# Attention scores from plain float32 queries and keys: two heads on the two row halves of the array, computed as one unit

## The chip, the cores and the metric

The kernel runs on one core of a Trainium2 chip. The metric is device time in microseconds, from the first to the last instruction of an execution and the little around it. The kernel before takes 2615.68 us (median of 3 executions, 2612.95 to 2617.23).

## The reference

One layer of a streaming encoder. 1024 frames of a new stream and 8 x 16 frames of running streams (together T = 1152 tokens, 9 tiles of 128) go through

    x = x + 0.5 * SwiGLU_1(RMSNorm(x))
    P = RMSNorm(x) @ w_in          # RWKV columns, and q, k, v of 8 attention heads of 64
    x = x + concat(RWKV7(P_rwkv), BandAttn(P_att)) @ w_out
    x = x + 0.5 * SwiGLU_2(RMSNorm(x));  y = RMSNorm_final(x)

What matters here is the attention. A chunk of 64 queries sees a band of keys, the 512 before it and its own 64:

    s = einsum('bhqd,bhkd->bhqk', q, k) * HEAD_DIM ** -0.5 + bias
    s = where(valid, s, -1e30);  p = softmax(s);  out = einsum('bhqk,bhkd->bhqd', p, v)

The running streams attend to a cache of 128 keys and to their own 16. Everything is float32; the last 512 keys and values are outputs as well. The RWKV part is a recurrence over time, so its chunks of 32 tokens must follow each other.

## The kernel before, in words

All large products are made in float32r, a float32 type that TensorE takes in one pass, with each operand split into a high part (rounded to float32r) and a low remainder; three products (high-high, high-low, low-high) stand for one.

The program has five stages. The first SwiGLU (lines 225 to 265). The projection `_project` (line 282), which for each of four pairs of heads projects the RWKV columns, prepares the RWKV chunks, and calls `_attention_in` (line 400) for that pair's q and k. Then `_attention_inputs` (line 355) projects v (`ps_av`, lines 377 to 379) while the RWKV recurrence already runs. Then attention and the rest of the recurrence side by side (lines 1167 to 1178). Then the output projection and the second SwiGLU.

`_attention_in` splits the projected q or k of a pair of heads (128 rows: two heads of 64) into high `qkh` (ScalarE, line 414) and low `qkl` (VectorE, line 415) and stores both to DRAM. A third, unsplit copy `qk` (VectorE, line 421) is made for the last third of q (the running streams) and the last two thirds of k; the keys that are an output are turned by TensorE into `ps_ko` (line 429) and copied out by ScalarE into `ko` (line 432).

`_attention_load` (line 881) loads a pair for attention, on GpSimd's DMA queue: per head a tile `kt` with the high part of the keys on rows 0 to 63 and the low part on rows 64 to 127, and tiles `q` of 384 tokens with the high part (and, apart, the low part) of the queries on both row halves. So the two float32r passes of line 941 contract over all 128 rows, and their sum is the full product. For the first pair the loads go in thirds.

An attention unit of the kernel before is one head and one tile of 128 queries, 72 in all (line 1014). `_attention_scores` (line 930) makes the scores `ps_s` in PSUM, adds the bias, takes the maximum (VectorE, line 963), the exponential `e` (ScalarE, line 966), and scales by the reciprocal sum (VectorE, line 968). `_attention_turn` (line 972) turns the probabilities by TensorE (`ps_pt`, line 980) and copies them to `ptr` on ScalarE. `_attention_out` (line 984) multiplies with v for both heads (`ps_o`, line 995). The units run in a software pipeline: scores of unit n, turn of unit n - 1, output of the pair before. The recurrence takes per chunk four groups of small products on TensorE: `ps_c` from `wout` (line 771), `ps_c` from `tt` (776), `ps_c` from `wst` (780, the new state) and `ps_yc` (784), with VectorE copies between (773, 778, 793).

The order on each engine isn't the order of the code: a scheduler puts the instructions of all these generators into one fixed list for each engine, which the engine works through in order. Pools of buffers add waits: a load into a buffer waits until its last reader is done. The SP queue carries the loads of weights and of the recurrence; GpSimd's queue carries attention's loads and stores, between GpSimd's own arithmetic for the recurrence (`y` at lines 833 and 841, `yo` at 853).

Of the kernel before, what the change touches and what calls it, by code (L numbers as in the profile page):

```python
# [395 lines left out]
def _attention_in(k, w, p, kind):  # L396
# [6 lines left out]
    def tile(dt, name):  # L403
        return k.io.tile([P, TG], dt, tag="ev", bufs=4, name=name)


    d = k.tc.dram_tile([2, 2, HD, T], F32, name=f"qk{kind}{p}")
    (k.kd if kind else k.qd)[p] = d
    for g in range(3):
        s = slice(g * TG, g * TG + TG)  # L410
# [19 lines left out]
        ko = tile(F32, "ko").rearrange("p (i h d) -> p i h d", h=2, d=HD)  # L430
        n = len(tiles)
        nc.scalar.activation(ko[:, :n].rearrange("p i h d -> p (i h d)"), tp[:, :n * P], AF.Copy)
# [442 lines left out]
def _attention_load(k, p):  # L875

    at = k.at
    dq = k.aq
    q = _K()

    q.ks = [at.tile([P, T], F32R, tag="kt", bufs=4, name="kt") for h in range(2)]
    q.v = at.tile([P, NT, P], F32, tag="v", bufs=2, name="v")

    q.bias = at.tile([P, 4, 256], F32, tag="bias", bufs=k.nbias, name="bias")
    q.qs = []
    for c in range(3):
        s = slice(TG * c, TG * c + TG)
        q.qs.append(at.tile([P, 2, 2, TG], F32R, tag="q", bufs=3, name="q"))
        for half in HEADS:
            dq.dma_start(q.qs[c][half].rearrange("d j h t -> d (j h) t").bitcast(F32),  # L890
                           k.qd[p][:, :, :, s].rearrange("j h d t -> d (j h) t"))
        if c == 0 or p == 0:
            cols = s if p == 0 else slice(0, T)
            for h in range(2):
                for j in range(2):
                    dq.dma_start(q.ks[h][HEADS[j], cols].bitcast(F32), k.kd[p][j, h, :, cols])
            i = slice(3 * c, 3 * c + 3) if p == 0 else slice(0, NT)
            dq.dma_start(q.v[:, i], k.vd[i, :, p * P:p * P + P].rearrange("i t d -> t i d"))
        if c == 0:
            dq.dma_start(q.bias, k.bias[p])  # L900
    return q


def _sample_load(k, p, a, q):
# [3 lines left out]
    qn = at.tile([P, 4, 2, NQ], F32, tag="qs", bufs=1, name="qs")  # L908
    k.aq.dma_start(qn.rearrange("p b e l -> p (b e l)"), k.qs[p])
    q.qz = at.tile([P, 4, 2, 2, NQ], F32, tag="z", bufs=1, name="qz")  # L910
    k.nc.gpsimd.memset(q.qz, 0.0)
    for e in range(2):
        k.nc.gpsimd.tensor_copy(q.qz[:, :, e, e], qn[:, :, e])
# [16 lines left out]
def _attention_scores(k, q, i, h):  # L930
# [4 lines left out]
    u = _K()  # L935
    u.q, u.i, u.h = q, i, h
    t = (i % 3) * P

    def scores(ps, c0, n):
        for j in range(2):  # L940
            mm(ps, q.qs[i // 3][:, j, h, t:t + P], q.ks[h][:, c0:c0 + n], start=j == 0, stop=j == 1)

    ps = k.psum.tile([P, 1024], F32, tag="s", bufs=2, name="ps_s")
    u.j0 = j0 = max(0, i - 4)
    if i < NPT:
        u.n = n = (i - j0 + 1) * P
        for c0 in range(0, n, 512):
            c1 = min(n, c0 + 512)
            scores(ps[:, c0:c1], j0 * P + c0, c1 - c0)
        w = min(n, 256)  # L950
        nc.vector.tensor_tensor(ps[:, n - w:n], ps[:, n - w:n], q.bias[:, h, 256 - w:], ALU.add)
        if i >= 4:
            nc.vector.memset(ps[64:128, 0:64], NEG)
    else:
        u.n = n = 2 * P
        for e in range(2):
            for b in range(4):
                mm(ps[32 * b:32 * b + 32, 0:P], q.qz[HEADS[h], b, e].rearrange("p e l -> p (e l)"),
                   q.kc[HEADS[h], 2 * b + e], start=e == 0, stop=e == 1)
        scores(ps[:, P:n], NPT * P, P)  # L960
        nc.vector.tensor_tensor(ps[:, :n], ps[:, :n], q.bias[:, 2 + h], ALU.add)
    nm = at.tile([P, 1], F32, tag="nm", bufs=4, name="nm")
    nc.vector.tensor_reduce(nm, ps[:, :n], AX.X, ALU.max, negate=True)
    u.e = at.tile([P, 5 * P], F32, tag="e", bufs=2, name="e")
    sm = at.tile([P, 1], F32, tag="sum", bufs=4, name="sum")
    nc.scalar.activation(u.e[:, :n], ps[:, :n], AF.Exp, bias=nm, accum_out=sm)
    nc.vector.reciprocal(sm, sm)
    nc.vector.tensor_scalar(u.e[:, :n], u.e[:, :n], sm, None, ALU.mult)
    return u
# [42 lines left out]
def _attention(k, a):  # L1012

    units = [(p, i, h) for p in range(NPAIR) for i in range(NT) for h in range(2)]
    done = []
    q = nq = None
    for n in range(len(units) + 2):
        if n < len(units):
            p, i, h = units[n]
# [221 lines left out]
```

## Time and profile before

| | us |
|---|---|
| median of 3 executions | 2615.68 |
| the profiled execution | 2614.86 |
| its span | 2613.1 |
| PE busy in it | 2508.2 (96%) |
| DVE busy | 1209.8 (46%) |
| ACT busy | 646.6 (25%) |
| GpSimd busy | 763.6 (29%) |

The span is read by stages. The two SwiGLU stages and the output projection (0 to 943 us and 1660 us to the end) hold nothing that the change touches. The stretch from 943 to 1261 us is the projection, 1261 to 1354 us that of v, 1354 to 1660 us attention beside the recurrence, of which the last 49 us (from 1611 us) are attention alone. TensorE's row says busy nearly everywhere, but the ends of its instructions are modelled, and its granted clock falls in the attention stretch, so there the starts of neighbouring instructions are the better measure of what one costs.

### The profile page before, as it was taken

To read this page: it belongs to the slowest core of one execution; us is meant where nothing else is said; L and a number is where in the kernel's file an instruction comes from. 1 tells how busy PE (TensorE), PEld (TensorE's weight loads), DVE (VectorE), ACT (ScalarE), POOL (GpSimd) and SP (SyncE) were. 2 spreads that over 40 slices of the span, in tenths; PEclk is the share of its full clock that TensorE was granted. 3 is DMA by queue.
4 is the path that set the end of the run, shared out by engine and by line. 5 is a ranking of instruction groups with operands and counts; after the bars stand their busy time and mean duration, and the time that the engine had idled before them with its cause. 6 is when DMAs were issued, how large, how long until landed. Compare 5 with 4: busy or idle time off the path is not lost.

```text
span 2613.1 us, 39575 instructions
## 1 busy us (share of the span) xinstructions
PE 2508.2 (96%) x16344; PEld 2270.1 (87%) x16344; DVE 1209.8 (46%) x2460; ACT 646.6 (25%) x1294; POOL 763.6 (29%) x686
## 2 busy tenths in 40 slices
PE   8999999999999899999997888899999999999998
PEld 8999999999999799989865666689999999999997
DVE  4432443244335443675856777513443344334435
ACT  5111111111111443344113345404111111111112
POOL 4222222222221343344114433103222222222221
PEclk9999999999999899999996889899999999999999
DMA  5311111111111234454669967301111111111111
GB/s 187 114 41 33 48 49 41 33 49 41 46 35 50 89 98 121 139 167 119 185 138 240 203 160 187 119 1 57 49 47 43 33 49 41 49 33 49 41 33 73
DMA packets 247798, 217.39 MB, mean 83 GB/s; under 512 B 54017, under 2 KB 218497, under 8 KB 247233
## 3 DMA queue, kind: packets, MB, share of 16 engines
q1 hardware_dynamic: 214252, 167.74, 22.1%
q0 software_dynamic: 7648, 25.43, 4.1%
q10 hardware_dynamic: 25716, 21.68, 2.7%
q8 instruction: 129, 2.11, 0.3%
q14 instruction: 53, 0.43, 0.1%
HBM read 155.35 MB, written 59.45 MB: 82 GB/s over the span
## 4 chain that ended last, share of the span: by engine, by line
PE 85%; DVE 6%; POOL 3%; issue 2%; ACT 1%; DMA 1%; SPq 0%; POOLq 0%; ACTq 0%; DVEq 0%
PE pg L218 7%; PE pg L220 7%; PE pg L219 7%; PE pu L218 7%; PE pu L220 7%; PE pu L219 7%; PE pd L256 7%; PE pd L258 7%; PE pd L257 7%; PE ps_p L220 2%; PE ps_p L219 2%; PE ps_p L218 2%; PE ps_wo L1071 1%; PE ps_wo L1070 1%; PE ps_wo L1069 1%
## 5 line engine op out<-in xcount | busy, mean ns | idle before, releaser
L156 POOL TENSOR_TENSOR spl<-raw,spl 128x1024 fp32r<-128x1024 f32 x166 | 399.5, 2409 | 796.8 <-ACT spl L155 796.7
L260 DVE TENSOR_TENSOR x<-pd,x 128x512 f32<-128x512 f32 x774 | 527.8, 691 | 7.0 <-PE pd L258 2.9
L244 DVE SCALAR_TENSOR_TENSOR hf<-pu,sl 128x384 f32<-128x384 f32 x132 | 73.6, 557 | 963.3 <-PE pu L220 949.0
L218 PE MATMUL pg<-xg,spl 128*128 128x384 f32 x1056 | 356.1, 337 | 0.0
L220 PE MATMUL pg<-xg,spl 128*128 128x384 f32 x1056 | 355.2, 336 | 0.0
L219 PE MATMUL pg<-xg,spl 128*128 128x384 f32 x1056 | 355.2, 336 | 0.0
L220 PE MATMUL pu<-xg,spl 128*128 128x384 f32 x1056 | 355.0, 336 | 0.0
L219 PE MATMUL pu<-xg,spl 128*128 128x384 f32 x1056 | 354.9, 336 | 0.0
L218 PE MATMUL pu<-xg,spl 128*128 128x384 f32 x1056 | 354.9, 336 | 0.0
L155 ACT ACTIVATE spl<-raw 128x1024 fp32r<-128x1024 f32 x166 | 174.8, 1057 | 628.5 <-PE pd L258 422.8
L256 PE MATMUL pd<-spl,h 128*128 128x512 f32 x792 | 310.6, 392 | 0.0
L258 PE MATMUL pd<-spl,h 128*128 128x512 f32 x792 | 310.4, 392 | 0.0
L257 PE MATMUL pd<-spl,h 128*128 128x512 f32 x792 | 310.4, 392 | 0.0
L247 POOL TENSOR_TENSOR h<-hf,h 128x384 fp32r<-128x384 f32 x132 | 134.1, 1016 | 589.3 <-ACT h L246 575.7
L218 PEld LDWEIGHTS pg<-xg,spl 128*128 128x128 f32 x1056 | 198.3, 188 | 1.8
L219 PEld LDWEIGHTS pg<-xg,spl 128*128 128x128 f32 x1056 | 198.4, 188 | 1.5
L220 PEld LDWEIGHTS pg<-xg,spl 128*128 128x128 f32 x1056 | 198.3, 188 | 0.0
L220 PEld LDWEIGHTS pu<-xg,spl 128*128 128x128 f32 x1056 | 198.2, 188 | 0.0
L218 PEld LDWEIGHTS pu<-xg,spl 128*128 128x128 f32 x1056 | 198.2, 188 | 0.0
L219 PEld LDWEIGHTS pu<-xg,spl 128*128 128x128 f32 x1056 | 198.2, 188 | 0.0
L258 PEld LDWEIGHTS pd<-spl,h 128*128 128x128 f32 x792 | 148.6, 188 | 33.7
L257 PEld LDWEIGHTS pd<-spl,h 128*128 128x128 f32 x792 | 148.5, 188 | 31.9
(227 smaller groups left out, 3656.0 us busy)
## 6 DMA issues: line engine op xcount, KB each, us to landing
raw<-in_w_ff_gate_dram SPq DMA_DIRECT2D x44, 512.0 KB
raw<-in_w_ff_up_dram SPq DMA_DIRECT2D x44, 512.0 KB
raw<-in_w_ff_down_dram SPq DMA_DIRECT2D x44, 512.0 KB
raw<-in_w_in_dram SPq DMA_DIRECT2D x26, 512.0 KB
q<-qk POOLq DMA_DIRECT2D x24, 384.0 KB, 8.0
ard<-ar SPq DMA_DIRECT2D x20, 256.0 KB
grd<-gram SPq DMA_DIRECT2D x20, 256.0 KB
wsd<-tb SPq DMA_DIRECT2D x20, 256.0 KB
```

The source lines that it names most:

```text
L155: k.nc.scalar.activation(dst[:, 0], raw, AF.Copy)
L156: k.nc.gpsimd.tensor_tensor(dst[:, 1], raw, dst[:, 0].bitcast(F32), ALU.subtract)
L218: mm(ps, w[:, 0, c], hi[:, c], start=c == 0, stop=False)
L219: mm(ps, w[:, 0, c], lo[:, c], start=False, stop=False)
L220: mm(ps, w[:, 1, c], hi[:, c], start=False, stop=c == KC - 1)
L244: nc.vector.scalar_tensor_tensor(hf, pu[:, :TG], 0.5, sl, ALU.mult, ALU.mult)
L247: nc.gpsimd.tensor_tensor(h[:, 1, s], hf, h[:, 0, s].bitcast(F32), ALU.subtract)
L256: mm(ps, ph[:, 0, a], pd[:, 0, b], start=j == 0, stop=False)
L257: mm(ps, ph[:, 0, a], pd[:, 1, b], start=False, stop=False)
L258: mm(ps, ph[:, 1, a], pd[:, 0, b], start=False, stop=j == len(pend) - 1)
L260: nc.vector.tensor_tensor(xs, ps, xs, ALU.add)
L1069: mm(ps, hi[:, c, s], ws[c][:, 0, b], start=c == 0, stop=False)
```

## The change

Queries and keys are no longer split. `_attention_in` makes one float32 tile `qk` on ScalarE, stores it once, and turns the output keys from the same tile; the copy of `ps_ko` moves to VectorE. `_attention_load` loads one tile of queries and one of keys for a pair of heads, head 0 on rows 0 to 63 and head 1 on rows 64 to 127; the tile of the running streams' queries is read from it, not loaded apart. `_attention_scores` makes both heads of a query tile in one unit: the code writes the two heads' products beside each other, each on its own 64 rows and into its own PSUM banks, and in plain float32 instead of two float32r passes. The probabilities `e` have 4 buffers instead of 2, q has 2 of 1152 tokens instead of 3 of 384 (split and doubled), kt 2 instead of 4.

```diff
 def _attention_in(k, w, p, kind):
...
-        hi, lo = tile(F32R, "qkh"), tile(F32R, "qkl")
-        nc.scalar.activation(hi, ps[:, :TG], AF.Copy, scale=scale)
-        nc.vector.scalar_tensor_tensor(lo, ps[:, :TG], scale, hi.bitcast(F32), ALU.mult, ALU.subtract)
-        for j, t in enumerate((hi, lo)):
-            k.aq.dma_start(d[j, :, :, s].rearrange("h d t -> (h d) t"), t.bitcast(F32))
-        if g == 0 or (g == 1 and kind == 0):
-            continue
-        raw = tile(F32, "qk")
-        nc.vector.tensor_scalar(raw, ps[:, :TG], scale, None, ALU.mult)
-        if kind == 0:
-            k.qs[p] = k.tc.dram_tile([P, P], F32, name=f"qs{p}")
-            k.aq.dma_start(k.qs[p], raw[:, 2 * P:])
+        raw = tile("qk")
+        nc.scalar.activation(raw, ps[:, :TG], AF.Copy, scale=scale)
+        k.aq.dma_start(d[:, g * TG:g * TG + TG], raw)
+        if g == 0 or kind == 0:
             continue
...
-        nc.scalar.activation(ko[:, :n].rearrange("p i h d -> p (i h d)"), tp[:, :n * P], AF.Copy)
+        nc.vector.tensor_copy(ko[:, :n].rearrange("p i h d -> p (i h d)"), tp[:, :n * P])
...
 def _attention_load(k, p):
...
-    q.qs = []
-    for c in range(3):
-        s = slice(TG * c, TG * c + TG)
-        q.qs.append(at.tile([P, 2, 2, TG], F32R, tag="q", bufs=3, name="q"))
-        for half in HEADS:
-            dq.dma_start(q.qs[c][half].rearrange("d j h t -> d (j h) t").bitcast(F32),
-                           k.qd[p][:, :, :, s].rearrange("j h d t -> d (j h) t"))
-        if c == 0 or p == 0:
...
+    for c in range(3 if p == 0 else 1):
+        cols, i = (slice(TG * c, TG * c + TG), slice(3 * c, 3 * c + 3)) if p == 0 else (slice(0, T), slice(0, NT))
+        dq.dma_start(q.q[:, cols], k.qd[p][:, cols])
+        dq.dma_start(q.k[:, cols], k.kd[p][:, cols])
+        dq.dma_start(q.v[:, i], k.vd[i, :, p * P:p * P + P].rearrange("i t d -> t i d"))
         if c == 0:
             dq.dma_start(q.bias, k.bias[p])
...
-def _attention_scores(k, q, i, h):
+def _attention_scores(k, q, i):
...
-    def scores(ps, c0, n):
-        for j in range(2):
-            mm(ps, q.qs[i // 3][:, j, h, t:t + P], q.ks[h][:, c0:c0 + n], start=j == 0, stop=j == 1)
...
+    def scores(p0, c0, n):
+        for u in us:
+            hs = HEADS[u.h]
+            mm(u.ps[:, p0:p0 + n], q.q[hs, i * P:i * P + P], q.k[hs, c0:c0 + n], start=True, stop=True)
...
-    u.e = at.tile([P, 5 * P], F32, tag="e", bufs=2, name="e")
...
+        u.e = at.tile([P, 5 * P], F32, tag="e", bufs=4, name="e")
...
 def _attention(k, a):
 
-    units = [(p, i, h) for p in range(NPAIR) for i in range(NT) for h in range(2)]
+    units = [(p, i) for p in range(NPAIR) for i in range(NT)]
...
+        yield
         if 0 <= n - 1 < len(units):
-            _attention_turn(k, done[n - 1])
-        if n >= 2 and units[n - 2][2] == 1:
-            _attention_out(k, units[n - 2][0], done[n - 3:n - 1])
+            for u in done[n - 1]:
+                _attention_turn(k, u)
+        if n >= 2:
+            _attention_out(k, units[n - 2][0], done[n - 2])
         yield
```

What the scheduler makes of it is seen at three places. The first is TensorE in the attention stretch, at the fifth or sixth tile of queries of the first pair of heads. The number behind `ps_s` is the PSUM tile, one for each head. Before, head 0 (13361) and head 1 (13385):

```order
L941 MATMUL ps_s_13361<-kt_12562,q_12583 128x512
L784 MATMUL ps_yc_13133<-mov_12705,wout_12707 32x64
L941 MATMUL ps_s_13361<-kt_12562,q_12583 128x512
L780 MATMUL ps_c_11193<-mov_12705,wst1_11190 64x64 x8
L784 MATMUL ps_yc_13133<-mov_12705,wout_12707 32x64 x5
L926 MATMUL ps_kc_13332<-ident_117,ck_12597 128x128 x4
L980 MATMUL ps_pt_13339<-ident_117,e_13303 128x128 x4
L941 MATMUL ps_s_13361<-kt_12562,q_12583 128x128
L771 MATMUL ps_c_11193<-mov_12705,wout_12707 32x64 x8
L941 MATMUL ps_s_13361<-kt_12562,q_12583 128x128
L980 MATMUL ps_pt_13345<-ident_117,e_13303 128x128
```

And the changed kernel there, head 0 (13186) and head 1 (13187):

```order
L969 MATMUL ps_pt_13155<-ident_117,e_12870 128x128
L928 MATMUL ps_s_13186<-kt_12459,q_12458 128x512
L928 MATMUL ps_s_13186<-kt_12459,q_12458 128x128
L969 MATMUL ps_pt_13161<-ident_117,e_12870 128x128
...
L984 MATMUL ps_o_13174<-ptr_12900,v_12460 64x128
L766 MATMUL ps_c_11089<-wx_12989,tt_12255 32x64 x8
L928 MATMUL ps_s_13187<-kt_12459,q_12458 128x512
L774 MATMUL ps_yc_13011<-mov_12566,wout_12568 32x64 x3
L928 MATMUL ps_s_13187<-kt_12459,q_12458 128x128
L770 MATMUL ps_c_11089<-mov_12566,wst1_11086 64x64 x8
```

One product now stands where two passes stood. The two heads, which the code writes beside each other, stand 20 rows apart here, with turns, outputs and a chunk's products between them.

The second place is GpSimd's list where attention begins. Before:

```order
L841 TENSOR_TENSOR y<-y,gn_s 128x512
L890 DMA q<-qk_7599 64x4x384
L853 TENSOR_TENSOR yo<-yo,gb 128x512
L833 TENSOR_TENSOR y<-y,gn_m 128x512
L890 DMA q<-qk_7599 64x4x384
L840 TENSOR_TENSOR gn_s<-gn_s,mhalf 128x8
L896 DMA kt<-qk_7702 64x384
L841 TENSOR_TENSOR y<-y,gn_s 128x512
L896 DMA kt<-qk_7702 64x384 x3
L898 DMA v<-vd 128x3x128
L900 DMA bias<-bias_1412 128x1024
```

And the changed kernel:

```order
L831 TENSOR_TENSOR y<-y,gn_s 128x512
L878 DMA q<-qk_7599 128x384
L879 DMA kt<-qk_7689 128x384
L880 DMA v<-vd 128x3x128
L882 DMA bias<-bias_1412 128x1024
L878 DMA q<-qk_7599 128x384
L879 DMA kt<-qk_7689 128x384
L843 TENSOR_TENSOR yo<-yo,gb 128x512
```

The loads of the first third, bias included, now stand ahead of `yo`, which waits for the recurrence; before, only half of the first queries did.

The third place is TensorE in the projection, where the output keys of the last pair of heads are turned (`ps_ko`). Before:

```order
L220 MATMUL ps_qk<-xg,spl 128x384
L624 MATMUL ps_g<-ar,kb 64x64 x16
L637 MATMUL ps_t<-ident,kb 128x128 x4
L583 MATMUL ps_k<-ident,rnb 128x128
L429 MATMUL ps_ko<-ident,qk 128x128 x2
L218 MATMUL ps_qk<-xg,spl 128x384
```

And the changed kernel:

```order
L220 MATMUL ps_qk<-xg,spl 128x384
L614 MATMUL ps_g<-ar,kb 64x64 x9
L419 MATMUL ps_ko<-ident,qk 128x128 x2
L218 MATMUL ps_qk<-xg,spl 128x384
L219 MATMUL ps_qk<-xg,spl 128x384
```

The turn comes sooner behind the projection it reads, since its input is now ready after one ScalarE instruction.

## Rows read from the trace of the kernel before

**Rows 1.** By stretch: busy us (instructions) of PE, PEld, DVE, ACT, POOL; PEclk; DMA share; GB/s.

```profile
943.00:1261.00 318.00, 302.52 (x2230) 284.13 (x2230) 200.28 (x518) 135.80 (x311) 132.30 (x184) 0.99 0.45 140
...
1354.00:1384.00 30.00, 17.17 (x294) 11.78 (x293) 13.96 (x40) 2.34 (x7) 11.65 (x15) 0.60 0.84 189
1384.00:1611.00 227.00, 197.36 (x2550) 136.41 (x2550) 171.67 (x473) 88.26 (x249) 93.99 (x112) 0.85 0.81 184
1611.00:1660.00 49.00, 42.52 (x464) 32.37 (x462) 34.10 (x98) 31.03 (x93) 5.99 (x11) 1.00 0.52 153
```

**Rows 2.** Groups of PE by line and shape: count, busy us, mean ns, idle before.

```profile
L941 PE MATMUL ps_s<-kt,q 128*128 128x512 f32 x80 | 35.3, 502 | 5.8 <-ACT e L966 5.6
...
L941 PE MATMUL ps_s<-kt,q 128*128 128x128 f32 x96 | 23.3, 296 | 6.2 <-DMA kt<-qk 6.2
...
L941 PE MATMUL ps_s<-kt,q 128*128 128x384 f32 x16 | 6.5, 480 | 0.3 <-ACT e L966 0.3
...
L941 PE MATMUL ps_s<-kt,q 128*128 128x256 f32 x16 | 5.3, 392 | 0.5 <-ACT e L966 0.5
```

**Rows 3.** Timeline of PE, 1290 us: start, us, what, releaser of idle time.

```profile
1290.52 0.28 PE L378 MATMUL ps_av<-spl,xg 128*128 128x256 f32 x1
1290.64 0.28 PE L379 MATMUL ps_av<-spl,xg 128*128 128x256 f32 x1
1290.85 0.43 PE L771 MATMUL ps_c<-mov,wout 96*32 96x64 f32 x16
1291.21 0.39 PE L377 MATMUL ps_av<-spl,xg 128*128 128x256 f32 x1
```

**Rows 4.** Chain that ended last, projection: start, us, what.

```profile
989.58 0.43 PE ps_gl L655 x2
...
1028.99 1.08 PE ps_g L624 x32
```

**Rows 5.** Chain that ended last, attention.

```profile
1455.00 0.60 PE ps_pt L980 x4
...
1463.29 1.24 PE ps_o L995 x20
```

**Rows 6.** Waits of PE, 1384 to 1611 us: who for whom, us, times, longest.

```profile
PE ps_pt L980 <- DVE e L968: 9.6, 9, 3.4
...
PE ps_s L941 <- ACT e L966: 4.5, 6, 1.5
...
PE ps_y L847 <- POOL y L841: 2.1, 1, 2.1
```

**Rows 7.** Timeline of PE where attention begins.

```profile
1354.66 0.69 PE L780 MATMUL ps_c<-mov,wst 128*64 128x64 f32 x16
...
1376.10 1.12 PE L780 MATMUL ps_c<-mov,wst 128*64 128x64 f32 x16
...
1384.03 0.66 PE L941 MATMUL ps_s<-kt,q 128*128 128x128 f32 x2 [6.24 <-DMA kt<-qk]
```

**Rows 8.** Timeline of POOL where attention begins.

```profile
1354.80 0.85 POOL L890 DMA_DIRECT2D q<-qk  x1 [1.93 <-PE ps_av L379]
1367.99 1.25 POOL L853 TENSOR_TENSOR yo<-yo,gb 128x512 f32<-128x512 f32 x1 [12.34 <-DVE yo L851]
...
1377.71 0.58 POOL L900 DMA_DIRECT2D bias<-bias  x1
```

**Rows 9.** Loads into the tile kt, from issue to landing.

```profile
DMA to landing us min/median/max: 3.6/8.5/12.2
```

**Rows 10.** Waits of POOL, 1384 to 1611 us.

```profile
POOL q L890 <- PE ps_s L941: 28.8, 5, 13.4
```

**Rows 11.** Waits of PE in the projection.

```profile
PE ps_ko L429 <- DVE qk L421: 7.3, 4, 2.4
```

**Rows 12.** Instructions on the tile ps_qk: count, ns min/median/max, first and last start.

```profile
L415 DVE SCALAR_TENSOR_TENSOR qkl<-ps_qk,qkh x24: 539/549/558, 960.8 to 1259.6; 128x384 fp32r<-128x384 f32 x24
L421 DVE TENSOR_SCALAR qk<-ps_qk x12: 536/544/551, 974.2 to 1260.1; 128x384 f32<-128x384 f32 x12
```

More of the change, by code (lines that the diff above doesn't have):

```diff
@@ L934, in _attention_scores @@
     at = k.at
-    u = _K()
-    u.q, u.i, u.h = q, i, h
-    t = (i % 3) * P
-    def scores(ps, c0, n):
-        for j in range(2):
-            mm(ps, q.qs[i // 3][:, j, h, t:t + P], q.ks[h][:, c0:c0 + n], start=j == 0, stop=j == 1)
-    ps = k.psum.tile([P, 1024], F32, tag="s", bufs=2, name="ps_s")
-    u.j0 = j0 = max(0, i - 4)
+    us = []
+    for h in range(2):
+        u = _K()
+        u.q, u.i, u.h = q, i, h
+        u.j0 = max(0, i - 4)
+        u.n = (i - u.j0 + 1) * P if i < NPT else 2 * P
+        u.ps = k.psum.tile([P, 1024], F32, tag="s", bufs=2, name="ps_s")
+        us.append(u)
@@ L945, in _attention_scores @@
+    def scores(p0, c0, n):
+        for u in us:
+            hs = HEADS[u.h]
+            mm(u.ps[:, p0:p0 + n], q.q[hs, i * P:i * P + P], q.k[hs, c0:c0 + n], start=True, stop=True)
+    n = us[0].n
     if i < NPT:
-        u.n = n = (i - j0 + 1) * P
         for c0 in range(0, n, 512):
[L948 to L951, printed above, removed]
@@ L952, in _attention_scores @@
-        if i >= 4:
-            nc.vector.memset(ps[64:128, 0:64], NEG)
+            scores(c0, us[0].j0 * P + c0, min(n, c0 + 512) - c0)
     else:
-        u.n = n = 2 * P
         for e in range(2):
             for b in range(4):
[L958 to L961, printed above, removed]
@@ L962, in _attention_scores @@
-    nm = at.tile([P, 1], F32, tag="nm", bufs=4, name="nm")
-    nc.vector.tensor_reduce(nm, ps[:, :n], AX.X, ALU.max, negate=True)
-    u.e = at.tile([P, 5 * P], F32, tag="e", bufs=2, name="e")
[L965 to L969, printed above, removed]
+                for u in us:
+                    hs = HEADS[u.h]
+                    mm(u.ps[32 * b:32 * b + 32, 0:P], q.qz[hs, b, e].rearrange("p e l -> p (e l)"),
+                       q.kc[hs, 2 * b + e], start=e == 0, stop=e == 1)
@@ new lines, in _attention_scores @@
+        scores(P, NPT * P, P)
+    for u in us:
+        ps = u.ps
+        if i < NPT:
+            w = min(n, 256)
+            nc.vector.tensor_tensor(ps[:, n - w:n], ps[:, n - w:n], q.bias[:, u.h, 256 - w:], ALU.add)
+            if i >= 4:
+                nc.vector.memset(ps[64:128, 0:64], NEG)
+        else:
+            nc.vector.tensor_tensor(ps[:, :n], ps[:, :n], q.bias[:, 2 + u.h], ALU.add)
+        nm = at.tile([P, 1], F32, tag="nm", bufs=4, name="nm")
+        nc.vector.tensor_reduce(nm, ps[:, :n], AX.X, ALU.max, negate=True)
+        u.e = at.tile([P, 5 * P], F32, tag="e", bufs=4, name="e")
+        sm = at.tile([P, 1], F32, tag="sum", bufs=4, name="sum")
+        nc.scalar.activation(u.e[:, :n], ps[:, :n], AF.Exp, bias=nm, accum_out=sm)
+        nc.vector.reciprocal(sm, sm)
+        nc.vector.tensor_scalar(u.e[:, :n], u.e[:, :n], sm, None, ALU.mult)
@@ L972, in _attention_turn @@
+    return us
 def _attention_turn(k, u):
@@ L1023, in _attention @@
                 _sample_load(k, p, a, q)
-            elif (i, h) == (4, 0) and p + 1 < NPAIR:
+            elif i == 4 and p + 1 < NPAIR:
                 nq = _attention_load(k, p + 1)
-            done.append(_attention_scores(k, q, i, h))
-            if h == 1 and i in (5, 6):
+            done.append(_attention_scores(k, q, i))
+            if i in (5, 6):
                 _sample_keys(k, q, 4 * (i - 5))
+        yield
         if 0 <= n - 1 < len(units):
-            _attention_turn(k, done[n - 1])
-        if n >= 2 and units[n - 2][2] == 1:
-            _attention_out(k, units[n - 2][0], done[n - 3:n - 1])
+            for u in done[n - 1]:
+                _attention_turn(k, u)
+        if n >= 2:
+            _attention_out(k, units[n - 2][0], done[n - 2])
         yield
@@ L1084, in tile_encoder_step @@
     k.nc, k.tc, k.o, k.dq, k.wq, k.aq = nc, tc, o, nc.sync, nc.sync, nc.scalar
-    k.qd, k.kd, k.qs, k.bias = {}, {}, {}, {}
+    k.qd, k.kd, k.bias = {}, {}, {}
     k.nraw, k.nspl, k.nt, k.nu = 3, 4, 20, 7
```

24 lines of the change are left out of this document (9 added, 15 removed).

## The prediction

> **What bounds the kernel now.** I first read busy time by stretch, since a share over the whole span says nothing here [rows 1]. The change touches three stretches. In the projection (943 to 1261 us) TensorE is busy 302.5 of 318 us at a granted clock of 0.99: TensorE bounds it, and only its few waits can be won. Where attention begins (1354 to 1384 us) TensorE has 17 us of work in 30, and the granted clock is 0.60. Beside the recurrence (1384 to 1611 us) it is busy 197 of 227 us at 0.85, and alone (1611 to 1660 us) 42.5 of 49 at 1.00. VectorE is the next busiest, 172 of 227 us. So in the attention stretch too the path runs through TensorE's list most of the time: what is added to that list adds to the time, except where it fills a wait. I then went to the waits of TensorE there, and to where each comes from [rows 6].
>
> **The scores, the largest term.** Before, the scores take 80 passes of 512 columns, 16 of 384, 16 of 256 and 96 of 128 [rows 2], which is 63,488 columns. A float32r pass of 256 columns starts 0.12 us behind the one before [rows 3], 0.47 ns a column, so they cost 29.8 us at the full clock. Plain float32 is in the trace too: one product of 256 columns of line 655 takes two records and 0.43 us [rows 4], 1.68 ns a column, thus 3.6 times a float32r pass. The changed kernel has one such product for each two passes, 31,744 columns: 53.3 us if each runs by itself. That is 23.5 us more.
>
> It would be nothing more if the two heads ran at the same time on their row halves, and the trace shows that halves can overlap: the 32 records of 64 columns of line 624, on alternating quarters, take 1.08 us [rows 4], 34 ns each, where 64 columns at half of 1.68 ns would take 54; the 20 records of 128 columns of line 995, on alternating column halves, take 1.24 us [rows 5], 62 ns against 107. But these stand beside each other in TensorE's list. The scores of the changed kernel don't: the scheduler takes head 1 when its PSUM tile is free, and puts turns, outputs and a chunk's products between the heads. In the whole list only six places have products of both heads next to each other, most of them of 128 columns. So I count the heads one after the other.
>
> By the order about two thirds of the turns (168 of 256) come before the recurrence's last chunk, so I put two thirds of the 23.5 us, 15.7, into the stretch with the granted clock of 0.85, where it becomes 18.4, and 7.8 us into the last one: 26 us. TensorE's waits in the mixed stretch for the probabilities (9.6 us) and for the exponential that frees a score tile (4.5 us) [rows 6] can be filled by longer scores and are eased by four buffers of `e`. I take 6 us of these 14 as cover. The term is +20 us; its bounds are 0 (the halves overlap, or all of it falls into waits) and +39 (no cover, and all of the mixed part at the half clock: 31.4 + 7.8).
>
> **Changes of the array's shape.** A recurrence product on 96 by 32 behind a full-array product starts 0.21 us after it, not 0.12 [rows 3]: 0.09 us for the change. Scores on 64 rows are a shape of their own; before they shared theirs with the turns. Counting neighbours of different shape in the two lists, from the start of the v projection, there are 572 changes instead of 533. 39 times 0.1 us is +4 us; bounds 0 and +9 (88 runs of scores at 0.1). The Trainium skill, TensorEngine Tiling (Array Packing), section Key Properties, says that a change of tiling mode drains the engine. It gives no price, and the 0.09 us here agrees that there is one; by the rule alone the sum would be the same with an unknown in place of the 4.
>
> **Where attention begins.** GpSimd issues half of the first queries at 1354.80 us, then waits 12.34 us for `yo`, which needs the recurrence, and issues `bias` only at 1377.71 [rows 8]. TensorE, with nothing but bare chunks, stands 6.24 us for `kt` and makes its first scores at 1384.03 [rows 7]. The changed list has q, kt, v and bias ahead of `yo`, without a wait on the recurrence between. With 8.5 us from issue to landing [rows 9] the keys are there about 1365 us, the bias a few us later. The list has 13 chunks ahead of the first scores instead of 14. A bare chunk takes 5.4 us (four from 1354.66 to 1376.10 us [rows 7]), so three bring the first scores to about 1371, 13 us sooner. One chunk of 5.4 us is only put off; among other work it costs perhaps 4. The term is -9 us; bounds -14 and 0, the latter if the loads collide, since DMA is busy 0.84 of that stretch [rows 1]. The queries' and keys' loads themselves shrink by more than half; no wait but the first one hangs on them, so past the start I count that at nothing.
>
> **The projection.** 24 instructions of 0.549 us and 12 of 0.544 us leave VectorE [rows 12], 19.7 us of its 200, and 8 copies of about half a us come. VectorE does not bound the stretch. What TensorE gains is the wait of `ps_ko` for the third tile of VectorE's queue, 7.3 us in four places [rows 11]. The new input comes from ScalarE alone, but the turn also stands closer behind its projection, with 9 small products between instead of 16 and 5. I take -6 us; bounds -9 (with the half clock that follows such a wait) and 0 (TensorE then runs ahead into the next wait on VectorE or GpSimd). 28 stores on ScalarE's queue go too; I count them at nothing, since TensorE has no wait there that hangs on them.
>
> **GpSimd's queue.** Loads of the next pair's queries wait 28.8 us for the last reader of a q buffer [rows 10] and hold up the recurrence's arithmetic behind them. With two whole q tiles the reader is long done. TensorE itself has waited 2.1 us for that arithmetic [rows 6]: -2 us, bounds -8 (waits that show under other names) and 0 (the stores of `am` block the queue next).
>
> **Sum.** +20 + 4 - 9 - 6 - 2 = +7 us. The profiled execution took 2614.86 us (span 2613.1), 0.8 below the median of 2615.68, so I predict 2622 us, 0.24% above the median. Two tenths of a per cent, 5.2 us, is about what a measurement of this kernel can tell from no change.
>
> **Rivals.** *The loads win.* The wait for the first keys is also what leaves TensorE half idle and at 0.60 of its clock. If, with the loads early, the list fills its waits better, half of the scores' cost is covered (+10), the start gives 14, the projection 9 and GpSimd 4, with 3 for the shapes: -14, or 2601 us. For it speaks that PE's waits in the mixed stretch and the start's are of the order of the added work; against it, that the waits are short and many. It decides once the cover passes 13 us. *The halves overlap after all.* Then the scores cost nothing more, and the sum is -13: 2602 us. The Trainium skill, TensorEngine Tiling (Array Packing), sections Theoretical Speedup and Key Properties, promises up to twice the speed for a contraction of 64 and independent tiles. The trace has overlap only between neighbours [rows 4, 5], and the list has few of them, so the change would not do what it says. *The added work meets a slow clock and a slow partner.* If the mixed part of the scores all runs at 1.2 GHz, the term is 39 without cover instead of 20; and alone, at the end, ten turns stand in a row in the new list, so that TensorE can wait for ScalarE's copies, some 3 us in all. 2622 + 19 + 3 is 2644 us.
>
> **How the numbers follow.** The forecast has 0.55, with a range of its own of 2610 to 2636; the loads 0.27; the overlap 0.05; the slow clock 0.13. Slower by over 0.2% (above 2621) is a bit over half of the forecast's part, 0.31, and all of the last, 0.13: 0.44 together. Within 0.2% is the rest of the forecast's part but its lower edge and the upper edge of the loads' case: 0.23. Faster has 0.33. The range, 2600 to 2643, reaches to the rivals on both sides; both signs hold much of the chance, since the terms are each larger than their sum.
>
> **What would show it.** By row: products of the scores of 512 columns that take about 0.43 us a record, two records each, at the full clock, and start one after the other (halved if the heads overlap); first scores 15 to 18 us behind the last product of v; no wait of `ps_ko` over 1 us; none of GpSimd's loads of q on TensorE; the last stretch, attention alone, about 0.7 us longer a query tile. The prediction is wrong if records of the two heads lie over each other, if the granted clock of the mixed stretch moves by more than a tenth, or if the projection ends over 10 us sooner or later.

## The result: 25 us slower, and where the time went

The changed kernel takes 2642.66 us (median of 4 executions, 2639.34 to 2644.83); the kernel before, on the same chip, 2616.45 us. The ratio is 1.0095, with a 95% interval of 1.0081 to 1.0110. The forecast was 2622 us, with 2643 us as the upper end of its range, and the time lies 0.3 us inside it.

The stretches of [rows 1] in the changed kernel's profile (span 2642.9 us):

```profile
943.00:1261.00 318.00, 299.17 (x2140) 280.67 (x2139) 176.67 (x451) 128.87 (x297) 126.26 (x178) 0.97 0.38 116
1354.00:1384.00 30.00, 25.75 (x409) 19.32 (x405) 16.50 (x46) 3.38 (x10) 8.69 (x10) 0.85 0.69 175
1384.00:1611.00 227.00, 216.10 (x2478) 133.77 (x2476) 159.85 (x457) 83.72 (x235) 72.62 (x76) 0.78 0.60 152
1611.00:1660.00 49.00, 42.98 (x415) 27.24 (x416) 34.27 (x91) 24.62 (x70) 17.65 (x17) 0.95 0.41 127
```

In the first stretch VectorE is busy 24 us less, yet TensorE gets through less: 2140 instructions instead of 2230. In the third TensorE is busier by 19 us and at a lower granted clock, 0.78 for 0.85. Milestones in the timelines of TensorE show where the delay comes in. Chunks of the recurrence are counted by the starts of `ps_c` from `wst`, from the first one behind 1280 us; the last two columns are experiments told below. Each column is one profiled execution; that of the third took 2618.2 us, while the ten executions of its kernel lie in two groups, five at 2617 to 2621 us and five at 2629 to 2630, and the last row goes by medians.

| start, us | before | changed | changed, old list | new list, VectorE's work kept |
|---|---|---|---|---|
| last product of q and k | 1258.7 | 1270.7 | 1260.7 | 1271.8 |
| chunk 1 | 1297.5 | 1313.8 | 1299.5 | 1316.0 |
| chunk 11 | 1358.9 | 1375.9 | 1360.9 | 1380.3 |
| first scores | 1384.0 | 1384.8 | 1371.1 | 1379.6 |
| chunk 40, the last | 1588.5 | 1624.6 | 1596.0 | 1632.0 |
| last attention output | 1659.6 | 1698.7 | 1672.5 | 1707.6 |
| output projection | 1666.7 | 1699.7 | 1673.5 | 1708.6 |
| run, against before | 1 | 1.0095 | 1.0026 | 1.0157 |

In the changed kernel 16 us are lost before attention has begun, 20 from there to the last chunk and 3 in the tail; 6 come back where the output projection starts and 4 in it (99.9 us from its first to its last product, 103.7 before). That leaves the 30 us between the two profiled executions; the medians are 26 apart.

**The scores.** Groups of TensorE by line and shape, as in [rows 2] (one product is two records now):

```profile
L928 PE MATMUL ps_s<-kt,q 64*128 64x512 f32 x80 | 59.8, 837 | 1.8 <-ACT e L955 1.7
...
L928 PE MATMUL ps_s<-kt,q 64*128 64x128 f32 x96 | 25.0, 378 | 0.0
L928 PE MATMUL ps_s<-kt,q 64*128 64x384 f32 x16 | 8.7, 632 | 0.0
L928 PE MATMUL ps_s<-kt,q 64*128 64x256 f32 x16 | 6.6, 499 | 0.5 <-ACT e L955 0.5
```

The counts are those foreseen (80 records of 512 columns for 80 passes), and a record's mean goes from 502 to 837 ns. The ends of records are modelled, so starts say more. One product of 512 columns at the full clock:

```profile
1431.12 1.12 PE L928 MATMUL ps_s<-kt,q 64*128 64x512 f32 x2 [0.29 <-ACT e L955]
```

The row behind it starts at 1432.18 us. That is 1.06 us, with a change of shape at both ends, where two records of 0.43 were foreseen and the changes of shape counted apart.

**The projection.** Waits of TensorE, 943 to 1261 us, one before and then those in the changed kernel:

```profile
PE ps_g L624 <- DVE kb L598: 6.9, 12, 1.0
...
PE ps_g L614 <- DVE kb L588: 14.4, 12, 2.7
PE ps_k L547 <- ACT sq L544: 3.3, 4, 2.8
PE ps_k L573 <- ACT rnb L571: 0.9, 1, 0.9
```

The wait of `ps_ko` [rows 11] is gone, as predicted. But `ps_g` now waits twice as long for `kb` of VectorE, up to 2.7 us at once, and one such wait is read through three timelines. TensorE (start, us, what, idle before and its releaser):

```profile
1033.82 0.33 PE L218 MATMUL ps_qk<-xg,spl 128*128 128x384 f32 x1
1034.00 0.33 PE L219 MATMUL ps_qk<-xg,spl 128*128 128x384 f32 x1
...
1037.65 1.97 PE L614 MATMUL ps_g<-ar,kb 64*64 64x64 f32 x32 [2.70 <-DVE kb L588]
...
1041.11 0.52 PE L220 MATMUL ps_qk<-xg,spl 128*128 128x384 f32 x1
1041.42 0.52 PE L218 MATMUL ps_qk<-xg,spl 128*128 128x384 f32 x1
```

VectorE, which makes `kb`:

```profile
1034.89 0.51 DVE L584 SCALAR_TENSOR_TENSOR sq<-sq,a 128x128 f32<-128x128 f32 x1 [2.87 <-POOL ar L582]
...
1037.21 0.29 DVE L588 TENSOR_TENSOR kb<-a,sg 128x128 f32<-128x128 f32 x1
```

GpSimd, which VectorE waits for:

```profile
1017.97 2.40 POOL L156 TENSOR_TENSOR spl<-raw,spl 128x1024 fp32r<-128x1024 f32 x1 [10.15 <-ACT spl L155]
1031.15 2.38 POOL L156 TENSOR_TENSOR spl<-raw,spl 128x1024 fp32r<-128x1024 f32 x1 [10.77 <-ACT spl L155]
1033.46 0.53 POOL L579 MEMSET ar<- 128x512 f32 x1
1033.93 0.53 POOL L580 MEMSET kb<- 128x512 f32 x1
1034.41 0.44 POOL L582 TENSOR_TENSOR ar<-sq,pt 128x128 f32<-128x128 f32 x1
```

And GpSimd in the kernel before, the same instructions for the same pair:

```profile
990.48 2.39 POOL L156 TENSOR_TENSOR spl<-raw,spl 128x1024 fp32r<-128x1024 f32 x1 [10.80 <-ACT spl L155]
992.80 0.53 POOL L589 MEMSET ar<- 128x512 f32 x1
993.27 0.53 POOL L590 MEMSET kb<- 128x512 f32 x1
993.75 0.44 POOL L592 TENSOR_TENSOR ar<-sq,pt 128x128 f32<-128x128 f32 x1
```

The memsets exist once a pair of heads, for the running streams. Before, they stood right behind the split of weights at 990.48 us; now three more splits (at 1005.43, 1017.97 and 1031.15 us, two are shown), each waiting some 10 us for ScalarE, stand ahead of them, and in TensorE's list `ps_g` stands ahead of the next products of `ps_qk`, which wait with it. The price is more than the wait, since the granted clock (third from the end of the row) then falls:

```profile
1037.60:1044.50 6.90, 6.85 (x52) 6.50 (x53) 2.83 (x9) 2.30 (x6) 1.88 (x3) 0.55 0.44 147
```

That is the lower level, 1.2 GHz, for most of 6.9 us: a pass of `ps_qk`, 0.18 us behind its neighbour ahead of the wait, comes 0.31 us behind it at 1041.42. The same happens at 1134 and 1226 us, and once with `ps_k` at 1070 us. The Trainium skill, TensorE: Matmul & The Clock Gate, section HAM oscillation, tells of this pattern for waits on DMA, a wait of the array and then work at the lower clock; these rows agree, with a wait on VectorE.

From the first to the last product of q and k, TensorE's idle time grows from 15 to 19 us, and the time at the lower clock from 3 to 20 us, which loses 10 us instead of 2. Together that is the 12 us by which the projection ends later, and two thirds of it are clock. Not every such wait is followed by the lower clock: before, `ps_ko` waited 2.2 to 2.4 us at three places, and the clock fell behind one of them (at 1254 us).

**Where attention begins.** GpSimd, as in [rows 8]:

```profile
1369.95 0.77 POOL L878 DMA_DIRECT2D q<-qk  x1
1370.73 0.54 POOL L879 DMA_DIRECT2D kt<-qk  x1
1371.26 0.79 POOL L880 DMA_DIRECT2D v<-vd  x1
1372.04 0.58 POOL L882 DMA_DIRECT2D bias<-bias  x1
```

The loads stand ahead of `yo`, one behind the other, and the first scores come at 1384.82 us without a wait, 16 us behind the last product of v (1368.7) instead of 30.

**The end.** TensorE before, and then in the changed kernel:

```profile
1658.68 1.12 PE L1003 MATMUL ps_o<-ptr,cv 128*64 128x16 f32 x29
1666.72 0.80 PE L1069 MATMUL ps_wo<-spl,xg 128*128 128x512 f32 x1 [6.92 <-ACT xg L1058]
```

```profile
1697.89 1.06 PE L992 MATMUL ps_o<-ptr,cv 128*64 128x16 f32 x32
1699.74 0.50 PE L1060 MATMUL ps_wo<-spl,xg 128*128 128x512 f32 x1 [0.79 <-ACT xg L1049]
```

### The profile page after: what moved, and what is told of

The parts are those of the page before. It is cut to its first block, busy times and chain, and to the rows that moved or that the text cites. A ratio compares the mean times of both kernels' runs of the same rounds, so it can differ in the third digit from the quotient of the medians.

```text
span 2642.9 us, 39395 instructions
## 1 busy us (share of the span) xinstructions
PE 2560.7 (97%) x16344; PEld 2286.2 (87%) x16344; DVE 1194.2 (45%) x2432; ACT 642.8 (24%) x1286; POOL 737.4 (28%) x646
## 4 chain that ended last, share of the span: by engine, by line
PE 48%; DVE 3%; issue 1%; ACT 1%; POOL 0%; POOLq 0%; DVEq 0%; ACTq 0%
PE pg L218 3%; PE pg L220 3%; PE pg L219 3%; PE pu L218 3%; PE pd L256 3%; PE pu L220 3%; PE pu L219 3%; PE pd L258 3%; PE pd L257 3%; PE ps_s L928 3%; PE ps_o L984 2%; PE ps_pt L969 2%; PE ps_yc L774 1%; PE ps_wo L1060 1%; PE ps_wo L1061 1%; PE ps_wo L1062 1%
```

## The experiments

Each set ran beside the kernel before on its chip (medians of 2615 to 2620 us), so gains and losses are given by the ratio to it, in us of 2616. "Old list" and "new list" are TensorE's lists in the projection, before and after the change.

**The projection part alone**, in front of the attention of before, which so counts its scores twice:

```diff
-        for j, t in enumerate((hi, lo)):
-            k.aq.dma_start(d[j, :, :, s]..., t.bitcast(F32))
+        raw = tile("qk")
+        nc.scalar.activation(raw, ps[:, :TG], AF.Copy, scale=scale)
+        for j in range(2):
+            k.aq.dma_start(d[j, :, :, g * TG:g * TG + TG]..., raw)
```

> Only the projection part of the change: one raw tile per group from ScalarE, the keys' output copy on VectorE, in front of the attention of before (it stores the same values as both parts, so the scores are those of unsplit values counted twice). Theory A (the new order of the projection's list costs time, since ps_g now stands where VectorE's kb is late): last query and key product 8 to 12 us later than before, waits of ps_g for kb of over 2 us as after the change, 2622 to 2629 us. Rival B (the projection only looks later because of a chance of the clock, and VectorE's saving is worth the 6 us of my prediction): no long waits of ps_g, 2606 to 2614 us.

Measured 2653.61 us, 1.0130 (1.0106 to 1.0154), +34 us. Theory A holds, and not far enough: the last query and key product comes at 1270.2 us, `ps_g` waits up to 2.7 us, chunk 1 starts at 1312.7 us, 15 us late; the other 19 us are lost behind it.

**The attention part alone**, behind the projection of before:

```diff
+    d = [k.tc.dram_tile([P, T], F32, name=f"qk{j}{kind}{p}") for j in range(2)]
+    (k.kd if kind else k.qd)[p] = d[0]
```

> Only the attention part: the projection of before, with split values and all its stores, in front of the attention of after, which reads the high parts alone (the low parts are left out of the scores). Theory A (plain float32 scores that stand singly in the list cost about 24 us of array time and the early start of attention gives little of it back): 2627 to 2640 us. Rival B (attention as predicted, about +13, and the projection is the rest): the same within 2625 to 2632, with the projection ending as before at 1259 us. Rival C (attention's cost comes from the projection's being late): not slower than 2619.

Measured 2633.28 us, 1.0045 (1.0024 to 1.0067), +12 us. The projection ends at 1260.6 us. Rival C falls. The ten executions lie between 2622 and 2640 us; their median is in the range of A alone, the 2628 us of the ratio in those of A and B alike, and +12 is near what the prediction had for attention, about +13. The two parts alone cost 34 and 12 us, 46 together, and the change that has both costs 25: they don't add up, so neither price is that of its part in the change.

**One float32r pass instead of plain float32**, all else as changed:

```diff
-    q.q = at.tile([P, T], F32, tag="q", bufs=2, name="q")
-    q.k = at.tile([P, T], F32, tag="kt", bufs=2, name="kt")
+    q.q = at.tile([P, T], F32R, tag="q", bufs=2, name="q")
+    q.k = at.tile([P, T], F32R, tag="kt", bufs=2, name="kt")
```

> The change with q and k read as float32r in one pass on the same row halves (the rounding is left as it comes), all else as changed. Theory A (the passes of plain float32 are the cost of the attention part): score products of 512 columns take 0.2 to 0.25 us in one record, the stretch from the last v product to the last attention output falls by 20 to 40 us against after, 2605 to 2622 us. Rival B (order and tiles of the new attention, units of both heads and fewer turns ahead of the last chunk, are the cost): less than 12 us is won, 2631 us or more.

Measured 2640.98 us (ten executions between 2619 and 2658), 1.0068 (1.0038 to 1.0098): 7 us below the change by the ratios, with intervals that overlap. That is rival B: 40 us of array time bring little here.

**Both heads in one PSUM tile:**

```diff
-        u.ps = k.psum.tile([P, 1024], F32, tag="s", bufs=2, name="ps_s")
+        if h == 0:
+            both = k.psum.tile([P, 2, 1024], F32, tag="s", bufs=1, name="ps_s")
+        u.ps = both[:, h]
```

> The change with both heads' scores in one PSUM tile, one buffer, so that the two heads' products stand next to each other in TensorE's list for most units. Theory A (row halves overlap where neighbours allow it): four records of 512 columns, two heads, in about 1.3 us instead of twice 0.93 at the full clock; about 15 us of array time is won, and the lost second buffer gives some of it back as waits for the exponential: 2628 to 2642 us. Rival B (halves of plain float32 don't overlap): four records in 1.7 us or more, and the time is 2643 us or above.

Measured 2690.88 us, 1.0268. Theory A is right on the halves, and wrong on the time. In this kernel, one head's 512 columns and then both heads' next to each other, both at about half clock (PEclk 0.50 and 0.56):

```profile
1417.18 2.07 PE L930 MATMUL ps_s<-kt,q 64*128 64x512 f32 x2
...
1460.41 2.01 PE L930 MATMUL ps_s<-kt,q 64*128 64x512 f32 x4
```

At the full clock, 512 and 128 columns of one head in the changed kernel, and then of both heads in this one. A row takes in all records that follow each other and names the first, so these are two records of 512 and two of 128 columns, and then four and four; in the second row the records of the two heads start 7 ns apart:

```profile
1455.94 1.34 PE L928 MATMUL ps_s<-kt,q 64*128 64x512 f32 x4
...
1665.16 1.35 PE L930 MATMUL ps_s<-kt,q 64*128 64x512 f32 x8 [1.58 <-ACT e L957]
```

Two heads take as long as one: the speedup of up to two that the Trainium skill gives for 64 rows (TensorEngine Tiling (Array Packing), section Theoretical Speedup) is there, for neighbours in the list. But with a single score tile TensorE waits, 1340 to 1700 us:

```profile
PE ps_pt L971 <- DVE e L959: 23.3, 17, 3.1
PE ps_s L930 <- ACT e L957: 12.1, 11, 1.7
```

In the changed kernel the same two waits are 1.4 and 2.2 us.

**The first score pass made twice, in the kernel before:**

```diff
-        for j in range(2):
-            mm(..., start=j == 0, stop=j == 1)
+        for f, j in enumerate((0, 0, 1)):
+            mm(..., start=f < 2, stop=f != 1)
```

> The kernel before with the first of the two score passes made twice, the first time for nothing (the output is unchanged): 31,744 more columns of TensorE work, 14.9 us at the full clock by the 0.47 ns of a float32r column, in a list that is otherwise the same. Theory A (array time in the attention stretch sets the time, as the prediction counted its scores): 2630 to 2640 us. Theory B (the stretch is set by the order of the list and by the clock that TensorE's waits bring down; more work fills waits and holds the clock up): within 5 us of the kernel before on the same chip, and the granted clock of the stretch from 1384 to 1660 us rises from 0.88 by 0.03 or more.

Measured 2633.44 us, 1.0067 (1.0052 to 1.0082), +17.5 us for 14.9 us of work. Theory A: in that list array time costs its whole length, within the interval of 14 to 21 us. The clock of the stretch doesn't rise, as theory B had it, but stays at 0.88.

**The change with the old list:** VectorE keeps a remainder and a second copy, from which the keys are turned, and ScalarE copies the turned keys out as before. This moves the scheduler back.

```diff
+        lo = tile("qkl")
+        nc.vector.scalar_tensor_tensor(lo, ps[:, :TG], scale, raw, ALU.mult, ALU.subtract)
         if g == 0 or kind == 0:
             continue
+        raw = tile("qkr")
+        nc.vector.tensor_scalar(raw, ps[:, :TG], scale, None, ALU.mult)
...
-        nc.vector.tensor_copy(ko[:, :n].rearrange("p i h d -> p (i h d)"), tp[:, :n * P])
+        nc.scalar.activation(ko[:, :n].rearrange("p i h d -> p (i h d)"), tp[:, :n * P], AF.Copy)
```

> The changed kernel with VectorE's work in the projection kept as before: a remainder that nobody reads and a second copy from which the keys are turned (both left out of what follows). The scheduler then gives TensorE the projection's list of before; the attention part is the changed one. Theory A (the saved VectorE work let the scheduler move ps_g ahead, and that costs what the projection lost): last query and key product at 1258 to 1262 us, no wait of ps_g for kb over 2.3 us, 2626 to 2636 us, faster than the changed kernel although VectorE does 20 us more. Theory B (the attention part alone makes the time): 2640 us or more.

Measured 2624.9 us, 1.0026 (1.0010 to 1.0041), +7 us: 18 us faster than the change, and a microsecond below the range of theory A; theory B falls. VectorE is busy 199.0 us from 943 to 1261 us, nearly as before (200.3). It has 24 instructions more than in the change, 13 us by an estimate from [rows 12] (32 of 0.55 us come back, 8 copies of about half a us go to ScalarE). Waits of TensorE, 943 to 1297 us:

```profile
PE ps_g L618 <- DVE kb L592: 8.7, 13, 1.8
PE ps_ko L423 <- DVE qkr L419: 8.0, 4, 2.7
```

`ps_ko` waits again, and it is the cheaper wait: the clock falls behind one of its three long ones. GpSimd's memset of `ar` is back, at 994.08 us.

**VectorE's work with the new list:** the remainder and all twelve copies of before go into a tile that nobody reads, so that the keys are turned from ScalarE's tile; VectorE copies the turned keys out, as in the change.

```diff
+        lo = tile("qkl")
+        nc.vector.scalar_tensor_tensor(lo, ps[:, :TG], scale, raw, ALU.mult, ALU.subtract)
+        if g == 2 or (g == 1 and kind):
+            nc.vector.tensor_scalar(lo, ps[:, :TG], scale, None, ALU.mult)
```

> The changed kernel with VectorE's 20 us of projection work kept (nobody reads the results), but the keys turned from ScalarE's tile as in the changed kernel, so that TensorE's list has ps_g ahead of ps_ko as there. Theory A (the place of ps_g in the list is what the projection lost by): VectorE being later, the waits of ps_g for kb grow, and the last query and key product comes at 1270 us or later; 2640 to 2660 us, against 2624.9 us for the kernel with the same VectorE work and the list of before. Theory B (VectorE having less to do made TensorE run ahead into waits, whatever the list): near 2625 us.

Measured 2656.86 us, 1.0157 (1.0126 to 1.0188), +41 us, with `ar` at 1032.17 us again and, 943 to 1300 us:

```profile
PE ps_g L618 <- DVE kb L592: 14.1, 12, 2.7
PE ps_k L551 <- ACT sq L548: 6.1, 4, 2.0
```

The time and the end of the projection are as theory A had them; the waits of `ps_g` did not grow (15.2 us in the change, in the same stretch). So the load of VectorE, even more of it than in the run before, doesn't bring the projection back, and theory B falls. The profiles of all runs say the same: in the five kernels here with the projection's list of before, up to small shifts, the memset of `ar` stands at 993 to 996 us and chunk 1 starts at 1299 to 1303; in the seven with the new list they stand at 1032 to 1036 and at 1312 to 1316. What isn't separated is which list it is: those of TensorE, VectorE and GpSimd change together, the last two runs also differ in the engine that copies the turned keys, and no run moves the memset alone.

**One head a unit, one pass, and both, behind either list.** Five more runs vary the unit (one head, as `_attention` was before) and the type, in the manner of the diffs above:

```diff
-    units = [(p, i) for p in range(NPAIR) for i in range(NT)]
+    units = [(p, i, h) for p in range(NPAIR) for i in range(NT) for h in range(2)]
```

New list, one head a unit, plain float32, and then one pass:

> The changed kernel with one head a unit again, as before the change: plain float32 scores, new loads and new projection stay. Theory A (plain float32 is the cost of the attention part): within 6 us of the changed kernel, 2637 to 2649 us. Theory B (units of both heads put the turns and outputs in bunches, so that engines wait for each other and the clock falls): 2615 to 2633 us.

> As the run before it, and q and k read as float32r in one pass (the rounding left as it comes): 40 us less array time than plain float32. Theory A (array time sets the time): 25 us or more below the kernel with one head a unit in plain float32. Theory B (waits and clock take what is saved, as in the one-pass kernel with units of both heads): within 12 us of it, with a lower granted clock in the stretch of attention beside the recurrence.

Old list, both heads a unit, one pass:

> The changed kernel with the projection's list of before (VectorE's extra work kept, nobody reads it) and with q and k read as float32r in one pass (the rounding left as it comes): 40 us less array time than the same kernel in plain float32, which took 2624.9 us. Theory A (with the projection in order, array time in the attention stretch counts, as the doubled pass in the kernel before did): 2590 to 2608 us, faster than both kernels. Theory B (in units of both heads the stretch waits for VectorE and ScalarE, and thinner work lowers the clock): 2617 to 2630 us, with a granted clock from the first score to the last output 0.05 or more lower than in plain float32.

Old list, one head a unit, plain float32, and then one pass:

> The kernel that has the changed attention behind the projection's list of before (VectorE's extra work kept, nobody reads it), with one head a unit instead of both: plain float32 scores, new loads. With both heads a unit it took 2624.9 us. Theory A (units of both heads save time by themselves, as the 18 us between these two forms behind the changed projection say): 2636 to 2648 us. Theory B (that difference came from the late projection, and single-head units are what the kernel before was ordered for): 2612 to 2625 us.

> As the run before it, with q and k read as float32r in one pass (the rounding left as it comes). With both heads a unit this took 2606.3 us. Theory A (array time counts behind the projection's list of before, and units of both heads save time): 15 to 25 us below the run before it, yet above 2606. Theory B (single-head units suit the list): 2590 to 2606 us, the fastest of all.

Measured 2660.37, 2659.99, 2606.30, 2651.30 and 2614.55 us. The first lies above both theories: units of both heads are no cost but a gain. The second is as theory B had it (granted clock 0.66 from the first score to the last output, 0.79 in plain float32). The third is as theory A had it, the fourth lies past theory A, and the fifth between the two, 37 us below the fourth.

Ratios to the kernel before (half-widths of the intervals 0.0015 to 0.0042):

| | new list | old list |
|---|---|---|
| both heads a unit, plain float32 | 1.0095 (the change) | 1.0026 |
| both heads a unit, one pass | 1.0068 | 0.9958 |
| one head a unit, plain float32 | 1.0166 | 1.0140 |
| one head a unit, one pass | 1.0159 | 0.9999 |

In the column of the old list array time counts: 18 and 37 us for 40 us of it; in that of the new one it brings 7 and 2 us, neither clear of the intervals. Across, the old list is worth 18, 29 and 42 us; the 7 us of one head a unit in plain float32 aren't clear of the intervals. Units of both heads are worth 11 to 30 us in each of the four pairs, a gain of the change for which I had no term. One kernel beats both: old list, units of both heads, one pass, 2606.3 us, 0.9958 (0.9935 to 0.9981). Its scores carry the rounding of q and k to float32r, which neither kernel has.

Why array time brings so little behind the new list is seen only in part. From the first score to the last output (columns as in [rows 1]), the kernel before:

```profile
1384.00:1659.60 275.60, 239.68 (x3012) 168.68 (x3012) 205.77 (x570) 119.13 (x340) 99.98 (x123) 0.88 0.76 179
```

The change:

```profile
1384.80:1698.70 313.90, 293.50 (x3126) 183.36 (x3122) 210.69 (x590) 124.38 (x347) 93.73 (x96) 0.79 0.54 145
```

The change with the old list:

```profile
1371.10:1672.50 301.40, 282.57 (x3110) 177.43 (x3106) 207.10 (x586) 123.78 (x347) 95.17 (x98) 0.82 0.58 152
```

One pass with the new list:

```profile
1383.70:1691.80 308.10, 269.03 (x3024) 180.22 (x3020) 213.50 (x590) 124.04 (x347) 94.56 (x96) 0.71 0.56 147
```

And with the old list:

```profile
1372.80:1658.60 285.80, 251.36 (x3006) 169.37 (x3004) 209.21 (x586) 123.35 (x347) 94.74 (x98) 0.76 0.60 159
```

The attention part alone, and then the projection part alone in front of the attention of before:

```profile
1371.30:1693.60 322.30, 298.58 (x3110) 183.55 (x3107) 209.81 (x586) 124.13 (x347) 94.50 (x98) 0.77 0.53 141
...
1393.70:1699.70 306.00, 264.40 (x3044) 186.42 (x3044) 202.56 (x572) 120.50 (x341) 101.80 (x126) 0.79 0.68 163
```

Busy time by granted clock, an estimate of the work at the full clock, is 191 us in both kernels with one pass, against 293.50 x 0.79 = 232 us in the change and 211 before. In the change 20 us of that stretch are idle and 62 are lost by the lower clock (busy time by one less the clock); before, it was 36 and 29. So the change brings 21 us of work, fills 16 us of waits and loses 33 us more by the clock, which makes the 38 us by which the stretch grows. Either part alone lowers the clock too: 69 us are lost with the attention part, 56 with the projection part, 51 in the change with the old list.

With one pass the work falls by 41 us. Behind the new list 39 us are then idle and 78 lost by the clock: more waits and a lower clock stay behind, and 35 of the 41 us go there. With the old list it is 34 and 60, against 19 and 51 in plain float32. What decides between the two isn't shown; in the traces about a fifth of TensorE's products of this stretch stand in another order.

## Why the prediction was wrong by 20 us

The forecast had 2622 us, and the time of 2642.66 is inside the range of 2600 to 2643 by luck: the upper end was set by a rival with another story, and no term of the prediction had the projection late.

**The projection (forecast -6, bounds -9 and 0).** This step failed. It took the list as it stood and subtracted the wait of `ps_ko`. The wait went; but the list had changed with it, GpSimd's as well, and I looked at neither beyond the rows around `ps_ko`. The nine small products ahead of the turn, "instead of 16 and 5", were the sign: work that stood ahead of the 216 products of the next pair had moved behind them. It cost 16 us at chunk 1. In the run it cost 18 us (1.0095 less 1.0026), and 34 us in front of the attention of before, so there is no one price. The runs say that this is the order and not VectorE's load: with that load kept, the old list gives 2 us at chunk 1, the new one 18.5. That the memset on GpSimd is the instruction that does it is read from the timelines of one pair, and wasn't tested by itself.

**The scores (+20).** The work was sized right: 23.5 us foreseen, 211 to 232 us measured by the estimate above. What becomes of it was not: the prediction let it fill 6 us of waits and lose about 3 us to the clock, and the stretch filled 16 and lost 33. What a microsecond of it costs depends on the list around it: all of it in the kernel before, a half to nine tenths behind the old list, and too little to be told from nothing behind the new one.

**The start (-9).** The scores begin 16 us behind the last product of v, within the 15 to 18 foreseen, and with the old list at 1371.1 us. In the change the late projection eats it. Its worth in time was not measured by itself, nor that of the changes of array shape (+4); the traces have 33 more of these, where 39 were counted.

**GpSimd's queue (-2).** GpSimd's loads of q wait 1.0 us in all, where they waited 28.8 [rows 10]. Part of the wait has only moved to the load behind them, 1384 to 1611 us:

```profile
POOL v L880 <- PE ps_o L988: 16.2, 2, 14.2
```

TensorE's wait for `y` is 1.8 us, where it was 2.1, so nothing shows the gain of 2. The sum of attention's own terms, 20 + 4 - 9 - 2 = +13, stands against +12 and +7 us in the two runs that have it without the new list. That such a sum fits doesn't show each of its terms: units of both heads, the clock and the 6 us at the end were not in it.

**The rivals.** 2642.66 us is the time that I gave to the slow clock and the slow partner, 2644. The clock did fall, in the mixed stretch from 0.85 to 0.78 and from the first score to the last output from 0.88 to 0.79. So this rival had hold of something that the forecast left out, though not at its size (the half clock throughout) and not by ScalarE's copies in the tail: TensorE's waits for `ptr` from 1611 us on are 3.6 us in all, where they were 2.5. Its cause isn't the late projection alone, since it falls behind the projection's list of before too (0.82 with the old list, 0.77 with the attention part alone). The overlap is real where the heads are neighbours, and the list has them so in few places, as was said.

**What the text named as proof of an error** came true twice: the projection ended 12 us later, over the 10 that I had set, and records of the two heads do lie over each other, if only in the six places (1384.82 us is the first) that the prediction had counted as neighbours.

## What to carry over

An engine relieved of work lets a scheduler move other engines' work: compare the lists of all engines over the whole stage, not around the edited instruction, and look for an instruction that has slid behind one that waits long (here, by the timelines, a memset behind three splits of weights on GpSimd). A wait of TensorE costs more than its length when the clock falls behind it: of the 38 us by which the attention stretch grew, 33 are the lower clock. The prices of two parts of a change need not add up (34 and 12 us, and 25 together). And in this kernel independent row halves overlapped only where the two products were neighbours in the list, which was no gain when the second buffer was given up for it.

## What was not expected of the hardware

Plain float32 products on the two row halves, next to each other, took 1.35 us where those on one half took 1.34 (512 and 128 columns, full clock), and 2.01 against 2.07 (512 columns) at about half clock. A wait of 2.70 us was followed by 6.9 us at a granted clock of 0.55. And 41 us less work on TensorE left the time where it was within 7 us, at a clock of 0.71 instead of 0.79.
